# Transposing query and key rows before they are split, two heads at a time

## The chip, the cores and the metric

The kernel runs on one core of a Trainium2 chip. Its engines work side by side: TensorE (PE in the profile; its weight loads are shown apart as PEld), VectorE (DVE), ScalarE (ACT), GpSimd (POOL), and SyncE (SP), whose queue issues the transfers. The metric is the device time of one execution in microseconds (us). Three runs of the kernel before took 1815.14 to 1818.62 us, with a median of 1815.4 us.

## The reference

Two layers of a generator work on 256 latent tokens and 256 context tokens of width 1024, in float32. Each layer is a half-step SwiGLU feed-forward, a token mixing and a second half-step feed-forward, each behind an RMS norm with a shift and a scale that come from a conditioning vector:

```python
x = x + 0.5 * mx[2] * swiglu(modulate(rms_norm(x), mx[0], mx[1]), *ffn1)
h = modulate(rms_norm(x), mx[3], mx[4])
y, y_c = mix_window_diff(...) if l % 2 == 0 else mix_mla_neighbourhood(...)
x = x + mx[5] * y
x = x + 0.5 * mx[8] * swiglu(modulate(rms_norm(x), mx[6], mx[7]), *ffn2)
```

Layer 0 mixes by windowed attention (8 query heads over 2 key heads) and differential attention (4 heads with two queries and keys each); layer 1 by latent attention (8 heads) and neighbourhood attention (8 heads). What matters here is how queries and keys come to the scores, in the windowed, the differential and the neighbourhood attention: each head of 64 columns is normed on its own, and for the latent tokens of layer 0 turned by a rotary embedding, and the score is the dot product of a query row with a key row:

```python
aq = apply_rope2d(rms_norm(aq.reshape(B, S, A_HEADS, HEAD_DIM), a_q_norm), *rope)
s = jnp.einsum('bqhgd,bkhd->bhgqk', qg, k).astype(jnp.float32) * (d ** -0.5)
```

## The kernel before

TensorE multiplies operands of type fp32r, a rounded form of float32. To keep the precision, the kernel splits an operand into a high part (the value rounded to fp32r, a copy on ScalarE) and a low part (value minus high part, on VectorE); `split` (lines 98 to 100) does both, and `mm3` (line 105) multiplies high by high, high by low and low by high. Weights come from memory in blocks `raw` and are split into `hs` by `wcols`; for 21 items named in the table `POOL` the low part is made by GpSimd instead (lines 275 and 276).

Activations stand transposed (features on partitions, tokens along the row) in `xT`. A projection such as `pbk` or `paq` gives two blocks of 128 tokens by four heads in PSUM. `head_norm` squares (ScalarE, line 619), sums (VectorE, line 621), takes the inverse root (line 128 and following, on both engines) and multiplies by it, and with gains and tables makes `tk`, on VectorE. `head_rows` then makes from `tk` the rows that the scores read: head dimension on partitions, tokens along the row. Since a head has only 64 columns, high part and low part of one head stand one above the other on the 128 partitions of one row tile, and one matmul over 128 partitions sums two of the products. A second tile of the keys holds the two halves swapped, for the other two products; queries need none.

Before, `head_rows` splits `tk` while tokens are still on partitions (line 651, two calls), then transposes high and low part of each head together (line 659, one transpose per head and token block, four of them into one PSUM bank of the tag `tr`, of which there are two), copies the bank to the row tile (line 664, or line 662 for the items in `ROWS_DVE`) and makes the swapped tile from the same bank (lines 667 and 669, or 671 for items that are not in `SWAP_ACT`). It runs 18 times with four heads and twice with two (`ak0`, `ak1`): 14 times in the mixing of layer 0, some 405 to 640 us, and 6 times in that of layer 1, some 1386 to 1600 us. The tile names are `bqt`, `bkt`, `aqt`, `akt`, `aktw`, `dqt`, `dkt`.

The items of a mixing stage are recorded in the order of a table written by hand (`MIX0`, `MIX1`). A scheduler then fixes each engine's order for good when the kernel is built, by when it takes the operands to be ready and buffers to be free; on the chip each engine takes its instructions in that order and waits where an operand isn't there.

The last feed-forward (layer 1) reads `hTl`: `raw_chunk` scales the rows of one chunk of `xT` (line 372) and splits them (line 373) as soon as the mixing has finished that chunk. Its first call also writes two columns 256 and 257 that hold the shift (lines 368 and 369), so that the same matmuls give the shift's part.

## Time and profile before

| | |
|---|---|
| median of three runs | 1815.4 us (1815.14 to 1818.62) |
| the profiled execution | 1815.7 us, span 1813.6 us |
| TensorE busy | 1762.3 us, 97% |
| VectorE busy | 1220.6 us, 67% |
| ScalarE busy | 738.8 us, 41% |
| GpSimd busy | 46.0 us, 3% |
| transfers | 256.9 MB, 142 GB/s on the mean |

The span runs from the first to the last instruction that the profiler saw; the execution's own time is 2.1 us longer. A busy time counts each moment once, even where instructions of one engine overlap, so that the mean duration of an instruction times its count can be more than the busy time. "Idle before" is what an engine waited ahead of a group of instructions, with the instruction that ended the wait. Granted clock is the share of TensorE's full 2.4 GHz that it was given in a stretch; its lower level is 1.2 GHz, 0.50.

### The profile page before, as it was taken

What the parts mean: (1) busy time and instruction counts of PE and PEld (TensorE: products, weight loads), DVE (VectorE), ACT (ScalarE), POOL (GpSimd) and SP (SyncE); (2) the same over time, 40 slices, a digit from 0 to 9 for tenths busy, and PEclk for the clock granted to TensorE, in tenths of its full rate; (3) what the DMA queues carried; (4) which work ended last, traced back from release to release, by engine and by line L of the source; (5) the groups of instructions that cost most, each with busy time, mean ns of one, the idle gap of its engine ahead of it and who ended that gap; (6) DMA issues with size and microseconds to landing.
All of it is one profiled execution on the core that took longest, in us unless ns stands there. A gap on an engine that the chain in (4) does not pass through costs nothing.

```text
span 1813.6 us, 26777 instructions
## 1 busy us (share of the span) xinstructions
PE 1762.3 (97%) x10563; PEld 1537.5 (85%) x10563; DVE 1220.6 (67%) x2343; ACT 738.8 (41%) x1322; POOL 46.0 (3%) x25
## 2 busy tenths in 40 slices
PE   7999999999999989999999999999999998999999
PEld 5788888898998888888888988888889986789998
DVE  5999953467688699989854633333346787876664
ACT  4333132345666543222233332222334656664442
POOL 0000000011010000000000000000001011000000
PEclk9999999999999989999999999999999999999999
DMA  9777752322110237778863233233233442155552
GB/s 305 273 245 225 236 190 88 116 73 68 50 60 14 59 121 240 241 229 261 300 199 105 81 94 94 92 105 103 88 111 101 89 102 57 47 178 183 175 186 82
DMA packets 214025, 256.90 MB, mean 142 GB/s; under 512 B 21484, under 2 KB 195724, under 8 KB 213900
## 3 DMA queue, kind: packets, MB, share of 16 engines
q1 hardware_dynamic: 213900, 255.19, 45.6%
q8 instruction: 83, 1.36, 0.3%
q14 instruction: 42, 0.34, 0.1%
HBM read 254.11 MB, written 1.05 MB: 141 GB/s over the span
## 4 chain that ended last, share of the span: by engine, by line
PE 87%; DVE 7%; ACT 3%; DMA 2%; issue 1%; SPq 0%; DVEq 0%; ACTq 0%
PE ups L103 23%; PE gps L103 23%; PE dps L103 23%; PE ops L103 3%; PE po L756 2%; PE sc L103 2%; DVE hs L100 1%; DMA bias<-in_d_rpb_dram 1%; PE trp L659 1%; PE pbk L103 1%; PE pbv L103 1%; PE paq L103 1%; PE pbq L103 1%; PE ptl L724 1%; PE mps L524 1%
## 5 line engine op out<-in xcount | busy, mean ns | idle before, releaser
L100 DVE TENSOR_TENSOR hs<-raw,hs 128x1024 fp32r<-128x1024 f32 (+2 forms) x308 | 367.9, 1200 | 284.1 <-ACT hs L99 283.4
L99 ACT ACTIVATE hs<-raw 128x1024 fp32r<-128x1024 f32 (+2 forms) x308 | 314.9, 1030 | 541.4 <-PE dps L103 177.8
L103 PE MATMUL dps<-ah,hs 128*128 128x512 f32 (+1 forms) x2256 | 401.0, 338 | 0.2 <-DVE hs L100 0.2
L103 PEld LDWEIGHTS dps<-ah,hs 128*128 128x128 f32 x2256 | 350.6, 190 | 46.4 <-DVE hs L100 0.4
L103 PE MATMUL gps<-hT,hs 128*128 128x512 f32 (+1 forms) x1680 | 375.3, 380 | 4.9 <-ACT hT L542 2.7
L103 PE MATMUL ups<-hT,hs 128*128 128x512 f32 (+1 forms) x1680 | 371.6, 377 | 0.0
L103 PEld LDWEIGHTS gps<-hT,hs 128*128 128x128 f32 x1680 | 305.0, 190 | 65.5 <-ACT hT L542 3.5
L103 PEld LDWEIGHTS ups<-hT,hs 128*128 128x128 f32 x1680 | 303.3, 188 | 58.8 <-issue 1.0
L212 DVE CUSTOM_DVE_ANT_0 junk<-mraw,cb,const 128x1024 f32<-128x1024 f32 x224 | 283.6, 1283 | 16.3 <-DMA mraw<-in_k_w_modT_dram 11.1
L99 ACT ACTIVATE ah<-af 128x512 fp32r<-128x512 f32 (+1 forms) x88 | 50.4, 574 | 127.5 <-DVE af L93 93.9
L295 DVE SCALAR_TENSOR_TENSOR xT<-dps,const,xT 128x256 f32<-128x256 f32 x112 | 50.3, 480 | 77.0 <-PE dps L103 76.9
L276 POOL TENSOR_TENSOR hs<-raw,hs 128x1024 fp32r<-128x1024 f32 (+2 forms) x21 | 45.8, 2186 | 1558.2 <-ACT hs L275 1493.8
L93 DVE TENSOR_TENSOR af<-sg,ups 128x512 f32<-128x512 f32 x66 | 45.2, 685 | 41.0 <-PE ups L103 40.9
L103 PE MATMUL gps<-hTl,hs 128*128 128x258 f32 x528 | 66.8, 284 | 1.6 <-DVE hTl L373 1.0
L428 ACT ACTIVATE sg<-gps 128x512 f32<-128x512 f32 x66 | 38.9, 589 | 70.2 <-PE gps L103 70.2
L103 PEld LDWEIGHTS gps<-hTl,hs 128*128 128x128 f32 x528 | 64.7, 190 | 2.5 <-DVE hTl L373 1.2
L103 PE MATMUL ups<-hTl,hs 128*128 128x258 f32 x528 | 65.5, 283 | 0.0
L103 PEld LDWEIGHTS ups<-hTl,hs 128*128 128x128 f32 x528 | 64.4, 190 | 0.0
L100 DVE TENSOR_TENSOR ah<-af,ah 128x512 fp32r<-128x512 f32 (+1 forms) x88 | 54.6, 621 | 13.2 <-ACT ah L99 13.2
L684 DVE TENSOR_REDUCE nm<-sc 128x1 f32<-128x512 f32 (+1 forms) x80 | 53.8, 682 | 5.0 <-PE sc L103 4.6
L690 ACT ACTIVATE pr<-sc,nm 128x512 f32<-128x512 f32 (+1 forms) x64 | 40.3, 634 | 13.7 <-DVE nm L684 13.4
L304 ACT ACTIVATE sq<-xT 128x256 f32<-128x256 f32 (+1 forms) x54 | 23.6, 449 | 50.9 <-DVE xT L295 50.6
(296 smaller groups left out, 1894.3 us busy)
## 6 DMA issues: line engine op xcount, KB each, us to landing
mraw<-in_k_w_modT_dram SPq DMA_DIRECT2D x128, 512.0 KB, 4.6
raw<-in_ffn_w_gate_dram SPq DMA_DIRECT2D x88, 512.0 KB, 4.7
raw<-in_ffn_w_up_dram SPq DMA_DIRECT2D x88, 512.0 KB, 4.5
raw<-in_ffn_w_down_dram SPq DMA_DIRECT2D x80, 512.0 KB, 4.1
raw<-in_cd_w_in_dram SPq DMA_DIRECT2D x18, 512.0 KB, 3.8
wm<-in_w_mod_dram SPq DMA_DIRECT2D x16, 512.0 KB, 8.7
raw<-in_ab_w_in_dram SPq DMA_DIRECT2D x16, 512.0 KB, 3.8
raw<-in_ffn_w_down_dram SPq DMA_DIRECT2D x16, 256.0 KB, 2.7
```

Of the source, the lines that this page charges most:

```text
L93: V.tensor_tensor(out=out_, in0=a, in1=b, op=ALU.mult)
L99: S.activation(h, src, AF.Copy)
L100: V.tensor_tensor(out=l, in0=src, in1=h.bitcast(F32), op=ALU.subtract)
L103: T.matmul(ps, a, b, start=start, stop=stop)
L212: V.tensor_tensor_reduce(out=junk, in0=raw, in1=mod_c[v], scale=0.5 if m in (2, 8) else 1.0, scalar=bT[:, l, m, k:k + 1], op0=ALU.mult, op ...
L276: nc.gpsimd.tensor_tensor(out=hs[:, 1, :n], in0=raw[:, :n], in1=hs[:, 0, :n].bitcast(F32), op=ALU.subtract)
L295: V.scalar_tensor_tensor(out=xT[dc][:, a:e], in0=ps[:, a:e], scalar=modT[:, l, v, m, dc:dc + 1], in1=xT[dc][:, a:e], op0=ALU.mult, op1=ALU ...
L304: S.activation(sq[:, cols], xT[dc][:, cols], AF.Square)
L428: S.activation(sg, g[:, :ntok], AF.Silu)
L684: V.tensor_reduce(out=nm[:, c], in_=view, axis=AX.X, op=ALU.max, negate=True)
L690: S.activation(p[:, cols], sc[:, cols], AF.Exp, bias=nm[:, i + b:i + b + 1], accum_out=den[:, i + b:i + b + 1])
L756: T.matmul(po[64 * x:64 * x + 64, q], val(x, c), pts[x][c], start=c == order[0], stop=c == order[-1], tile_position=(0, 64 * x))
```

## The change

`head_rows` no longer splits `tk`. It transposes `tk` itself, two neighbouring heads (128 columns) at a time, one transpose per pair of heads and token block; all of a call's transposes go into one PSUM bank. After a transpose the first head of a pair stands on partitions 0 to 63, the second on 64 to 127. For each of the two (x), the high part is copied from PSUM to the same partitions of the row tile, and VectorE subtracts it from PSUM into the other half. The second head of a pair so has its high part on the upper 64 partitions, where the first has its low part there, in queries and keys alike. The swapped tile is now copied from the row tile in SBUF, one head and one half at a time, no longer from PSUM.

In `raw_chunk` the first chunk's scaling is issued first, and the shift columns' copies are ordered behind it (`issue_after`).

```diff
         if not hraw:
             hraw.append(hp.tile([P, KC, 2, 264], R32, tag="hTl", name="hTl", bufs=1))
+        h, x, sc = hraw[0][:, k, :, 0:256], xT[k][:, 0:256], modT[:, l, 0, m + 1, k:k + 1]
+        first = S.activation(h[:, 0], x, AF.Copy, scale=sc).ins
+        if len(hraw) == 1:
+            hraw.append(first)
             sh = modT[:, l, 0, m, :].rearrange("p (k o) -> p k o", o=1)
             for c in (256, 257):
-                S.activation(hraw[0][:, :, 0, c:c + 1], sh, AF.Copy)
+                with tc.issue_after(first):
+                    S.activation(hraw[0][:, :, 0, c:c + 1], sh, AF.Copy)
                 V.tensor_tensor(out=hraw[0][:, :, 1, c:c + 1], in0=sh, in1=hraw[0][:, :, 0, c:c + 1].bitcast(F32),
                                 op=ALU.subtract)
-        h, x, sc = hraw[0][:, k, :, 0:256], xT[k][:, 0:256], modT[:, l, 0, m + 1, k:k + 1]
-        S.activation(h[:, 0], x, AF.Copy, scale=sc)
...
-        head_norm(tv, src, gain, rope, sq)
-        spf = []
-        for b in range(2):
-            sp = sq if b == 0 else w2("sp")
-            spv = sp[:, :nh * P].rearrange("p (h s e) -> p h s e", s=2, e=HD)
-            split(spv[:, :, 0, :].bitcast(R32), spv[:, :, 1, :].bitcast(R32), tv[:, b])
-            spf.append(sp)
+        head_norm(tk[:, :2 * nh * HD].rearrange("p (b h e) -> p b h e", b=2, e=HD), src, gain, rope, sq)
+        pt = bank("tr", "trp")
         for i in range(nh // 2):
-            pt = bank("tr", "trp")
+            for b in range(2):
+                T.transpose(pt[:, 256 * i + b * P:256 * i + (b + 1) * P], tk[:, (b * nh + 2 * i) * HD:(b * nh + 2 * i + 2) * HD],
+                            idm)
+        for i in range(nh // 2):
+            d = dst_of(i)
             for x in range(2):
-                for b in range(2):
-                    h = 2 * i + x
-                    T.transpose(pt[:, 256 * x + b * P:256 * x + (b + 1) * P], spf[b][:, P * h:P * h + P], idm)
-            rows = pt.rearrange("p (x n) -> p x n", x=2)
-            if now[0] in ROWS_DVE.split():
-                V.tensor_copy(dst_of(i), rows)
-            else:
-                S.activation(dst_of(i), rows, AF.Copy)
+                own, other = (slice(0, 64), slice(64, 128))[::1 - 2 * x]
+                r = pt[own, 256 * i:256 * i + 256]
+                if now[0] in ROWS_DVE.split():
+                    V.tensor_copy(d[own, x], r)
+                else:
+                    S.activation(d[own, x], r, AF.Copy)
+                V.tensor_tensor(out=d[other, x], in0=r, in1=d[own, x].bitcast(F32), op=ALU.subtract)
             if swap_of is not None:
-                d = swap_of(i)
-                S.activation(d[0:64], rows[64:128], AF.Copy)
-                if now[0] in SWAP_ACT.split():
-                    S.activation(d[64:128], rows[0:64], AF.Copy)
-                else:
-                    V.tensor_copy(d[64:128], rows[0:64])
+                e = swap_of(i)
+                for x in range(2):
+                    own, other = (slice(0, 64), slice(64, 128))[::1 - 2 * x]
+                    S.activation(e[other, x], d[own, x].bitcast(F32), AF.Copy)
+                    if now[0] in SWAP_ACT.split():
+                        S.activation(e[own, x], d[other, x].bitcast(F32), AF.Copy)
+                    else:
+                        V.tensor_copy(e[own, x], d[other, x].bitcast(F32))
```

The scheduler orders the changed program anew. On TensorE, at the start of the first mixing stage, this is the order of before, from the first key projection (`pbk`; `pbv` and `pbq` are other projections, `trp` the transposes; x69 is 69 in a row):

```order
L103 MATMUL pbk<-hs,hT 128x256 x69
L103 MATMUL pbv<-hw,hT 128x256 x15
L103 MATMUL pbk<-hs,hT 128x256 x2
L103 MATMUL pbv<-hw,hT 128x256
L659 MATMUL trp<-const,hsq 128x128 x2
L103 MATMUL pbv<-hw,hT 128x256
L659 MATMUL trp<-const,sp 128x128
L659 MATMUL trp<-const,hsq 128x128
L659 MATMUL trp<-const,sp 128x128 x2
L659 MATMUL trp<-const,hsq 128x128
L659 MATMUL trp<-const,sp 128x128
L103 MATMUL pbv<-hw,hT 128x256 x2
```

Behind these stand 25 of `pbk`, 29 of `pbv` and 6 of `pbq` up to the second group of eight transposes, then 65 of `pbq` up to the third. On TensorE, from the same projection on, the changed kernel has:

```order
L103 MATMUL pbk<-hs,hT 128x256 x68
L103 MATMUL pbv<-hw,hT 128x256 x5
L655 MATMUL trp<-const,tk 128x128 x4
L103 MATMUL pbk<-hs,hT 128x256
L103 MATMUL pbv<-hw,hT 128x256 x7
L103 MATMUL pbk<-hs,hT 128x256 x2
L103 MATMUL pbv<-hw,hT 128x256 x17
L103 MATMUL pbk<-hs,hT 128x256 x25
L103 MATMUL pbv<-hw,hT 128x256 x19
L103 MATMUL pbq<-hs,hT 128x256 x5
L655 MATMUL trp<-const,tk 128x128 x4
L103 MATMUL pbq<-hs,hT 128x256 x28
```

The groups have four transposes in place of eight; the first stands 14 projection matmuls earlier, the second 1, and the third, which follows the last row, 38.

On VectorE, this is what stood before, from the product that begins the norm of the second rows (`ht<-pbk`) to their split (`hsq`, `sp`; `hs<-raw` is a weight block):

```order
L93 TENSOR_TENSOR ht<-pbk,hrs 128x512
L100 TENSOR_TENSOR hs<-raw,hs 128x1024
L93 TENSOR_TENSOR hsq<-ht,const 128x512
L93 TENSOR_TENSOR tk<-ht,const 128x8x16 x4
L96 TENSOR_TENSOR tk<-tk,hsq 128x512
L100 TENSOR_TENSOR hsq<-tk,hsq 128x4x64
L100 TENSOR_TENSOR sp<-tk,sp 128x4x64
```

And this stands on VectorE at the same place now (`bqt` are the rows of the call before, line 666 their low parts):

```order
L666 TENSOR_TENSOR bqt<-trp,bqt 64x256
L663 CAST bqt<-trp 64x256
L93 TENSOR_TENSOR ht<-pbk,hrs 128x512
L666 TENSOR_TENSOR bqt<-trp,bqt 64x256
L93 TENSOR_TENSOR hsq<-ht,const 128x512
L93 TENSOR_TENSOR tk<-ht,const 128x8x16 x4
L100 TENSOR_TENSOR hs<-raw,hs 128x1024
L96 TENSOR_TENSOR tk<-tk,hsq 128x512
```

The split is gone from the end, the weight block has moved to just before the last sum, and low parts of the preceding rows stand between the steps of the norm.

On ScalarE, at the end of the second mixing stage, before (`const<-xT` and `sq` are squares for the next norm):

```order
L275 ACTIVATE hs<-raw 128x1024
L301 ACTIVATE const<-xT 128x256
L372 ACTIVATE hTl<-xT,const 128x256
L304 ACTIVATE sq<-xT 128x256
L372 ACTIVATE hTl<-xT,const 128x256
```

and on ScalarE at this place in the changed kernel:

```order
L275 ACTIVATE hs<-raw 128x1024
L301 ACTIVATE const<-xT 128x256
L367 ACTIVATE hTl<-xT,const 128x256
L373 ACTIVATE hTl<-const 128x8 x2
L304 ACTIVATE sq<-xT 128x256
L367 ACTIVATE hTl<-xT,const 128x256
```

The two shift columns have come here from a place in the first feed-forward stage behind layer 0's mixing; VectorE's two subtractions for them stand around the first chunk's in the same way. On SyncE's queue, in the second mixing stage, one block of `c_w_uq` now stands in front of twelve transfers of `bias` and not behind them.

## Rows read from the trace of the kernel before

**Rows 1.** The page's first part: busy time, share of the span and instructions of each engine.

```profile
PE 1762.3 (97%) x10563; PEld 1537.5 (85%) x10563; DVE 1220.6 (67%) x2343; ACT 738.8 (41%) x1322; POOL 46.0 (3%) x25
```

**Rows 2.** The page's fourth part: the chain of work that ended last, share of the span by engine.

```profile
PE 87%; DVE 7%; ACT 3%; DMA 2%; issue 1%; SPq 0%; DVEq 0%; ACTq 0%
```

**Rows 3.** Busy times in the two mixing stages: start and end, length, then busy time and count of PE, PEld, DVE, ACT and POOL, the granted clock, the share of the transfers, GB/s.

```profile
405.00:640.00 235.00, 226.86 (x1729) 208.17 (x1729) 182.57 (x465) 145.08 (x354) 12.89 (x6) 0.99 0.18 55
1386.00:1600.00 214.00, 199.53 (x1398) 172.00 (x1397) 163.38 (x420) 134.22 (x334) 20.91 (x10) 0.98 0.37 86
```

**Rows 4.** Who TensorE waited for between 385 and 1625 us: us in total, times, longest.

```profile
PE trp L659 <- DVE hsq L100: 9.7, 7, 2.4
PE kvt L1107 <- DVE ckv L1103: 4.8, 1, 4.8
```

**Rows 5.** The transposes of line 659: shortest, median and longest duration in ns, first and last start.

```profile
L659 PE MATMUL trp<-const,hsq x76: 270/273/448, 417.2 to 1472.4; 128*128 128x128 f32 x76
...
L659 PE MATMUL trp<-const,sp x76: 270/273/421, 417.5 to 1472.5; 128*128 128x128 f32 x76
```

**Rows 6.** The chain that ended last in order of time, first mixing stage: start, length in us, what.

```profile
427.91 1.94 PE trp L659 x8
...
447.62 0.87 PE trp L659 x8
...
572.76 0.87 PE trp L659 x8
```

**Rows 7.** Groups of instructions by shape, ScalarE: line, output and input, shapes, count, busy us and mean ns of one, idle time before.

```profile
L99 ACT ACTIVATE ah<-af 128x256 fp32r<-128x256 f32 x22 | 9.1, 412 | 33.4 <-DVE af L437 30.2 <-PE ups L103 3.2
L99 ACT ACTIVATE hsq<-tk 128x256 fp32r<-128x256 f32 x18 | 7.4, 413 | 19.7 <-DVE tk L93 10.2 <-DVE tk L96 9.5
...
L99 ACT ACTIVATE ckt<-cktr 96x256 fp32r<-96x256 f32 x16 | 5.4, 374 | 1.6 <-PE cktr L1213 1.6
L664 ACT ACTIVATE dkt<-trp 128x512 fp32r<-128x512 f32 x8 | 4.8, 598 | 2.6 <-PE trp L659 2.5
...
L667 ACT ACTIVATE dkt<-trp 64x512 fp32r<-64x512 f32 x8 | 4.8, 595 | 0.1
```

**Rows 8.** The same, VectorE.

```profile
L100 DVE TENSOR_TENSOR hsq<-tk,hsq 128x256 fp32r<-128x256 f32 x18 | 9.0, 498 | 1.9 <-ACT hsq L99 1.9
L100 DVE TENSOR_TENSOR sp<-tk,sp 128x256 fp32r<-128x256 f32 x18 | 7.5, 419 | 0.0
...
L100 DVE TENSOR_TENSOR ckt<-cktr,ckt 96x256 fp32r<-96x256 f32 x16 | 6.1, 412 | 0.7 <-ACT ckt L99 0.6
L710 DVE TENSOR_SCALAR pra<-pra,rd 128x256 f32<-128x256 f32 x14 | 4.7, 346 | 0.0
L671 DVE CAST dkt<-trp 64x512 fp32r<-64x512 f32 x6 | 4.1, 684 | 4.1 <-ACT dkt L667 4.1
...
L100 DVE TENSOR_TENSOR sp<-tk,sp 128x128 fp32r<-128x128 f32 x2 | 0.6, 290 | 0.0
L100 DVE TENSOR_TENSOR hsq<-tk,hsq 128x128 fp32r<-128x128 f32 x2 | 0.6, 285 | 0.0
```

**Rows 9.** VectorE's instructions in order of time: start, us, what, and idle time before with its releaser.

```profile
413.15 0.89 DVE L93 TENSOR_TENSOR tk<-ht,const 128x128 f32<-128x128 f32 x4
...
423.02 3.10 DVE L93 TENSOR_TENSOR tk<-ht,const 128x128 f32<-128x128 f32 x4
426.16 0.69 DVE L96 TENSOR_TENSOR tk<-tk,hsq 128x512 f32<-128x512 f32 x1
427.34 0.42 DVE L100 TENSOR_TENSOR hsq<-tk,hsq 128x256 fp32r<-128x256 f32 x1 [0.48 <-ACT hsq L99]
```

**Rows 10.** TensorE's instructions in order of time, at three places.

```profile
427.91 0.66 PE L659 MATMUL trp<-const,hsq 128*128 128x128 f32 x2 [2.12 <-DVE hsq L100]
...
538.91 0.44 PE L659 MATMUL trp<-const,hsq 128*128 128x128 f32 x2 [2.45 <-DVE hsq L100]
...
1614.55 3.51 PE L103 MATMUL gps<-hTl,hs 128*128 128x258 f32 x24 [1.02 <-DVE hTl L373]
```

**Rows 11.** GpSimd's instructions in order of time, at two places.

```profile
422.77 2.60 POOL L276 TENSOR_TENSOR hs<-raw,hs 128x1024 fp32r<-128x1024 f32 x1 [31.86 <-ACT hs L275]
...
1466.39 2.42 POOL L276 TENSOR_TENSOR hs<-raw,hs 128x1024 fp32r<-128x1024 f32 x1 [0.45 <-ACT hs L275]
```

**Rows 12.** Busy times in three short stretches, with the columns of rows 3.

```profile
420.00:430.00 10.00, 7.88 (x59) 7.71 (x58) 8.31 (x15) 4.07 (x7) 2.60 (x1) 0.88 0.37 105
...
540.00:550.00 10.00, 10.00 (x71) 9.63 (x69) 7.61 (x19) 5.83 (x16) 0.00 (x0) 0.83 0.09 27
...
1600.00:1618.00 18.00, 16.58 (x132) 15.81 (x131) 18.00 (x36) 12.56 (x24) 2.40 (x1) 1.00 0.38 123
```

**Rows 13.** VectorE's casts of line 662, one form: durations in ns, first and last start.

```profile
L662 DVE CAST dqt<-trp x2: 679/680/680, 1467.5 to 1468.8; 128x512 fp32r<-128x512 f32 x2
```

**Rows 14.** The shift columns, lines 368 and 369, with the columns of rows 13.

```profile
L368 ACT ACTIVATE hTl<-const x2: 202/210/217, 906.6 to 906.7; 128x8 fp32r<-128x8 f32 x2
...
L369 DVE TENSOR_TENSOR hTl<-const,hTl x2: 169/169/169, 908.8 to 908.9; 128x8 fp32r<-128x8 f32 x2
```

**Rows 15.** The transfers of `bias`: time in SyncE's queue for one in ns, and how long VectorE waited for them (us, times).

```profile
L1053 SPq DMA_DIRECT2D bias<-in_d_rpb_dram x32: 601/615/1879, 1416.6 to 1494.5; - x32
...
  DMA bias<-in_d_rpb_dram: 6.6, 3
```

1 line of the change is left out of this document (removed).

## The prediction

> **What bounds the kernel now.** I read the page's busy times first: TensorE is busy for 1762.3 of 1813.6 us, VectorE for 67% and ScalarE for 41% [rows 1]. Then the chain that ended last: 87% of it is TensorE work, 7% VectorE, 3% ScalarE [rows 2]. So a microsecond of TensorE work is worth nearly a microsecond wherever no other wait stands behind it, and work on the other two engines is worth something only where TensorE waits for it. The change lies in the two mixing stages, so I asked for these two stretches alone. From 405 to 640 us TensorE is busy 226.86 of 235 us and VectorE 182.57; from 1386 to 1600 us TensorE has 199.53 of 214 us, VectorE 163.38 [rows 3]. Both are still TensorE stages, but with VectorE at 78% and 76% close behind. The waits of TensorE say who it waits for there: the longest entry is the very place of the change, the transposes of query and key rows (`trp`) behind the second half of the split on VectorE: 9.7 us, 7 times [rows 4].
>
> **Transposes.** `head_rows` runs 18 times on four heads and twice on two. Each run made two transposes per head, one per token half: 18 x 8 + 2 x 4 = 152, which the trace shows as 76 + 76 [rows 5]. Two heads now go through one transpose, so 76 stay and 76 go, with their weight loads. Eight of them in a row take 0.87 us in the chain at full clock, 0.109 us each; right behind a wait the same eight took 1.94 us, 0.24 each [rows 6]. At 0.109: 52 fewer in the first mixing stage, 5.7 us, and 24 fewer in the second, 2.6 us. I count them by the share of these stages in which TensorE has work (96.5% and 93.2%, [rows 3]): 5.5 + 2.4 = **-7.9 us**. Ends: 0, if the next instruction waits anyway, and -18 (76 x 0.24).
>
> **The split.** What goes on ScalarE: 40 copies of 64 columns by four heads (36 at 0.40 to 0.41, 4 at about 0.3: 15.9 us), 33 row copies of 512 columns at 0.598 (19.7) and 25 swap copies at 0.595 (14.9), in all 50.5 us. What comes: 66 copies of 64x256 out of PSUM, which the trace shows nearly so as `ckt<-cktr` 96x256 at 0.374 (24.7), and 50 swap copies of 64x256 from SBUF, nearest `ah<-af` 128x256 at 0.412 (20.6), in all 45.3 [rows 7]. ScalarE loses 5 us; it is 62% busy in both stages, so this counts as 0.
>
> On VectorE 40 subtractions go (9.0 + 7.5 + 1.2 us, by the busy times) and 16 casts of 512 columns at 0.684 (10.9): 28.6 us. There come 76 subtractions out of PSUM, 6.1 us for 16 in `ckt<-cktr`, 0.38 each (29.0), 10 copies out of PSUM, taken at the same 0.38 (3.8), and 22 swap copies of 64x256 inside SBUF. No row shows those; the nearest is the scaling of 128x256 in place, 4.7 us for 14, 0.336 each (7.4) [rows 8]. That is 40.2 us, so VectorE gains **11.6 us** of work, some 8 of it in the first stage. What hides it is TensorE's own work on projections and outputs; VectorE then stands at about 81% and 78%. Cost on the path: between 0 and +11.6; I take **+1.0**, nearer to 0, because the new work stands behind the transposes, not in front of them, and its readers, the scores, come 9 (last key item of the second stage) to 63 matmuls (first stage) later in TensorE's order.
>
> **The wait before the transposes.** In the trace of before, the sum `tk` ends at 426.85 and the transposes start at 427.91: 1.06 us for copy and subtraction, which no longer stand between [rows 9, 10]. That would be 7 x 1.06 = 7.4 us if every such wait shrank. I take 0, with -7.4 as the other end. The order is why: TensorE's queue is fixed, and the transposes have been moved forward in it. Counted from the first `pbk` matmul, the three first groups stood behind 87, 150 and 215 projection matmuls and now stand behind 73, 149 and 177. Where they arrive earlier, they ask earlier for `tk`. At the second place `tk` itself isn't earlier: the weight split `hs` (1.23 us) that stood in front of the chain now stands inside it, before the last sum, and four subtractions with four copies of the preceding rows (8 x 0.38 = 3.0 us) replace two subtractions and two casts (2.2 us) ahead of it.
>
> What stretched that chain is elsewhere. Four products `tk<-ht` took 3.10 us at 423.02 and 0.89 us at 413.15 [rows 9]; a GpSimd subtraction ran from 422.77 to 425.37 [rows 11], and the 2.12 us wait of TensorE follows; the same stands at 538.91 with 2.45 us [rows 10]. After both, the granted clock is a mixture of its two levels of 2.4 and 1.2 GHz: 0.88 in 420 to 430 and 0.83 in 540 to 550 us [rows 12]. The change doesn't touch the GpSimd instructions, so I leave these two waits and their clock as they are.
>
> A stretched chain can also befall the new instructions. A cast out of PSUM wasn't stretched: two `dqt<-trp` took 0.68 us each at 1467.5 and 1468.8 [rows 13] while GpSimd worked from 1466.39 to 1468.81 [rows 11]. By these rows the 76 new subtractions and 16 lost casts are of the unstretched or half unstretched kind, and the 22 swap copies, now SBUF to SBUF, of the exposed kind. GpSimd works for 33.8 of 449 us in the two stages [rows 3], 7.5%, so one or two of 22 copies would meet it, at most 2.4 us each, and three of the 40 removed subtractions no longer do: taken as 0. The Trainium skill, "SBUF — State Buffer", section "SBUF: two separate sides", says that a VectorE instruction in a two-port mode or with two SBUF inputs and a GpSimd instruction lock each other out of a shared port for a whole instruction; that speaks against the swap copies, and the stretched `tk<-ht` agrees with it. By that rule alone the sum would stay within 2 us of mine, in either direction.
>
> **The shift columns.** Two ScalarE instructions (0.21 each) and two on VectorE (0.169) move from 907 us to 1606 us [rows 14], behind the first chunk. From 1600 to 1618 us VectorE has no idle time at all, 18.00 of 18 us [rows 12], and TensorE waits for its last result, 1.02 us at 1614.55 [rows 10]. Two instructions more in that row of work are 0.34 us on the path; taken with their overlap as **+0.3**, ends 0 and +0.8 (all four). At 907 us their absence is worth nothing, since TensorE is the bound there.
>
> **Transfers.** On SyncE's queue one weight load moves ahead of twelve bias transfers (0.615 us each to issue). VectorE waited 6.6 us in three waits for such a transfer [rows 15] without holding TensorE for it. Cost 0, ends -1 and +2.
>
> **Sum.** The profiled execution took 1815.7 us (1813.6 of span and 2.1 around it). 1815.7 - 7.9 + 1.0 + 0.3 = 1809.1. The median shown is 1815.4, 0.3 lower, so I predict **1808.8 us**.
>
> **Rivals.** B: the waits go too. For it: the seven waits are real and 1.06 us of each was the split. Against it: the moved transposes and GpSimd. With four of seven shortened (4.2 us) and one low-clock stretch gone (0.17 of 10 us, 1.7) and no cost on VectorE: 1815.4 - 7.9 - 5.9 + 0.3 = 1802.
>
> C: given back. TensorE arrives 7.9 us earlier at work that VectorE's unchanged chains finish when they did, as at `kvt`, where it waited 4.8 us for VectorE [rows 4]. Then the time stays: 1815.4 + 0.3, about 1815.7. Against it: TensorE's idle time is only 8.1 and 14.5 us in the two stages, so most of its work has no such wait behind it.
>
> D: slower. VectorE becomes the engine that TensorE waits for: the head norms form one chain on it, and the next norm queues behind the subtractions of the preceding rows. If all of the 11.6 us falls in front of a waited result: 1815.4 + 11.6 - 7.9 + 0.3 = 1819.4. It decides as soon as VectorE adds over 8 us to these chains. For it: stretches such as 1600 to 1618 us, where VectorE has no gap. Against it: on average it keeps a fifth free in the mixing stages.
>
> **How the numbers follow.** I give my forecast 0.55 (1805.5 to 1812.5), B 0.15, C 0.17, D 0.13. What this kernel's measurement can tell from no change is 0.2%, 3.6 us, so faster means below 1811.8. Faster: 0.50 of mine and B, 0.65. Same: 0.05 of mine, 0.15 of C, 0.03 of D, 0.23. Slower: 0.02 of C and 0.10 of D, 0.12. The range of 1800 to 1817 takes in B and C and leaves out D and the best end of B.
>
> **What would show it.** Right: 76 `trp` matmuls; TensorE's idle time in the two mixing stages about as before and the stages together some 7 us shorter; the subtraction near 0.41 us and the swap copy inside SBUF near 0.35; the last stream's first matmuls waiting for VectorE a few tenths longer. Wrong: `trp` waits gone (B), new TensorE waits on the subtraction or behind `kvt` and `cqtr` that make up for the transposes (C), or VectorE above 90% in the mixing stages with longer stages (D).

## The result and the profile after

The changed kernel takes 1842.5 us, median of 4 runs (1840.8 to 1843.1), against 1815.4 for the kernel before: a ratio of 1.0144, 95% interval 1.0126 to 1.0161. It is 27 us slower; 1808.8 had been predicted, in a range to 1817. In its profiled execution the page shows the following.

```profile
PE 1773.3 (96%) x10487; PEld 1533.3 (83%) x10487; DVE 1241.4 (67%) x2395; ACT 739.4 (40%) x1340; POOL 45.7 (2%) x25
...
PE 81%; DVE 12%; ACT 3%; DMA 2%; issue 1%; SPq 1%; POOL 0%; DVEq 0%; ACTq 0%
```

TensorE issues 76 matmuls fewer and is busy 11 us longer than in [rows 1]; in the chain that ended last VectorE's share went from 7% [rows 2] to 12%. To see where the time went, I cut both executions at the same instructions: the first `pbq` matmul, the first `gps` of the feed-forward part behind it, the first `pdq`, the first `gps` of the last stream. Five stretches, lengths in us from the start times in the traces:

| kernel | to pbq | mixing 1 | feed-forward | mixing 2 | last |
|---|---|---|---|---|---|
| before | 399.1 | 255.4 | 731.9 | 225.6 | 201.7 |
| changed | 402.5 | 261.6 | 737.7 | 237.3 | 201.8 |

So 18 us were lost in the mixing stages, where 7.9 were to be gained, and 9 us in feed-forward parts that the change doesn't touch. The busy times of the two mixing stages of the changed kernel, and of 200 us of pure feed-forward work, columns as in [rows 3]:

```profile
402.50:664.10 261.60, 237.11 (x1771) 213.60 (x1769) 216.97 (x547) 155.44 (x390) 12.35 (x6) 0.98 0.20 59
1401.80:1639.10 237.30, 215.47 (x1470) 186.13 (x1469) 180.27 (x464) 143.29 (x356) 23.45 (x11) 0.96 0.35 85
...
1100.00:1300.00 200.00, 200.00 (x874) 163.55 (x873) 67.07 (x78) 51.24 (x61) 0.00 (x0) 1.00 0.31 95
```

The same stretches of the kernel before:

```profile
399.10:654.50 255.40, 239.41 (x1822) 219.83 (x1821) 202.08 (x515) 156.00 (x380) 12.89 (x6) 0.98 0.20 60
1386.40:1611.90 225.50, 211.03 (x1493) 183.50 (x1493) 174.88 (x443) 141.79 (x346) 23.16 (x11) 0.98 0.37 89
...
1100.00:1300.00 200.00, 200.00 (x884) 165.59 (x883) 68.03 (x77) 52.10 (x61) 0.00 (x0) 1.00 0.32 97
```

The last row of each is the one to look at twice: TensorE is busy all the time at full clock in both, yet it gets 874 matmuls done in 200 us and not 884. A busy share of 100% hides that some of the matmuls are a little slower. The groups by shape name them, and show the new instructions (TensorE, ScalarE, VectorE):

```profile
L103 PE MATMUL gps<-hT,hs 128*128 128x512 f32 x1488 | 351.3, 393 | 3.8 <-ACT hT L545 2.7 <-DVE hs L100 1.1
...
L655 PE MATMUL trp<-const,tk 128*128 128x128 f32 x76 | 12.9, 293 | 12.0 <-DVE tk L96 5.7 <-DVE tk L93 4.7 <-DVE nm L690 1.4
...
L665 ACT ACTIVATE aqt<-trp 64x256 fp32r<-64x256 f32 x16 | 6.1, 378 | 9.3 <-PE trp L655 4.8 <-DVE aqt L666 4.5
...
L666 DVE TENSOR_TENSOR aqt<-trp,aqt 64x256 fp32r<-64x256 f32 x16 | 6.8, 422 | 1.8 <-ACT aqt L665 1.4
...
L675 DVE CAST dkt<-dkt 64x256 fp32r<-64x256 f32 x12 | 3.5, 289 | 0.4
```

`gps` was 346.5 us and 390 ns before; with `ups` the 512-column matmuls on `hT` cost 10.4 us of TensorE more. The transposes went from 18.6 + 16.7 [rows 5, by busy time] to 12.9 us. Of the waits of TensorE, those that answer to [rows 4]:

```profile
PE kvt L1111 <- DVE ckv L1107: 5.7, 1, 5.7
PE trp L655 <- DVE tk L96: 5.7, 5, 2.6
PE trp L655 <- DVE tk L93: 4.7, 5, 1.7
...
PE pdq L103 <- DVE hs L100: 3.4, 1, 3.4
```

The wait before the transposes stayed (9.7 before, 11.8 in three entries now, the third 1.4 behind `nm`), and a new one is there, `pdq` (a projection of the second mixing stage) behind a weight split on VectorE. So three things had to be explained: the slower feed-forward matmuls, the `pdq` wait, and the mixing stages.

### The profile page after: what moved, and what is told of

Its sections match the earlier page's. It is cut to its first block, busy times and chain, and to the rows that moved or that the text cites. A ratio compares the mean times of both kernels' runs of the same rounds, so it can differ in the third digit from the quotient of the medians.

```text
span 1841.0 us, 26711 instructions
## 1 busy us (share of the span) xinstructions
PE 1773.3 (96%) x10487; PEld 1533.3 (83%) x10487; DVE 1241.4 (67%) x2395; ACT 739.4 (40%) x1340; POOL 45.7 (2%) x25
## 4 chain that ended last, share of the span: by engine, by line
PE 81%; DVE 12%; ACT 3%; DMA 2%; issue 1%; SPq 1%; POOL 0%; DVEq 0%; ACTq 0%
PE ups L103 23%; PE gps L103 23%; PE dps L103 22%; PE ops L103 2%; PE po L760 2%; DVE hs L100 2%; PE sc L103 1%; DVE nm L688 1%; DMA bias<-in_d_rpb_dram 1%; DVE tk L93 1%; PE pdv L103 1%; PE ptl L728 1%; DVE hT L355 1%; PE mps L527 1%; PE paq L103 1%
## 5 line engine op out<-in xcount | busy, mean ns | idle before, releaser
L103 PE MATMUL gps<-hT,hs 128*128 128x512 f32 (+1 forms) x1680 | 379.7, 382 | 4.9 <-ACT hT L545 2.7
L103 PE MATMUL ups<-hT,hs 128*128 128x512 f32 (+1 forms) x1680 | 377.0, 380 | 0.0
L212 DVE CUSTOM_DVE_ANT_0 junk<-mraw,cb,const 128x1024 f32<-128x1024 f32 x224 | 283.6, 1280 | 16.1 <-DMA mraw<-in_k_w_modT_dram 11.9
L103 PE MATMUL gps<-hTl,hs 128*128 128x258 f32 x528 | 66.7, 284 | 1.8 <-DVE hTl L376 1.0
```

The costliest lines, as they stand in the source:

```text
L103: T.matmul(ps, a, b, start=start, stop=stop)
L212: V.tensor_tensor_reduce(out=junk, in0=raw, in1=mod_c[v], scale=0.5 if m in (2, 8) else 1.0, scalar=bT[:, l, m, k:k + 1], op0=ALU.mult, op ...
```

## Experiments

Ratios are against the kernel before, run on the same chip, with 95% intervals. Stage lengths are those of the one execution that was profiled. It can lie 4 us from its kernel's median (e8: 1825.6 against 1829.6), so a stage difference of 2 or 3 us shows little by itself. Byte addresses are the places that the builds gave the tiles; the traces hold none.

**The shift columns alone, and the place of the streamed tiles.** First the smaller of the two edits, by itself (e1).

```diff
 # before, with raw_chunk of the changed kernel
+        first = S.activation(h[:, 0], x, AF.Copy, scale=sc).ins
...
             for c in (256, 257):
-                S.activation(hraw[0][:, :, 0, c:c + 1], sh, AF.Copy)
+                with tc.issue_after(first):
+                    S.activation(hraw[0][:, :, 0, c:c + 1], sh, AF.Copy)
```

> The kernel before with the edit of the shift columns alone; every engine has the order of before, but for the two copies and two subtractions of those columns. What else differs is where tiles lie in on-chip memory: the eight tiles of normalized stream (hT) lie at 121,696 bytes and above in a partition before, and four of the eight lie at 16,512 to 32,895 bytes here, as they do in the changed kernel. Theory A (a 512-column matmul that streams from that low stretch takes longer: 234 ns from start to start in the changed kernel's trace, 226.7 elsewhere): the four feed-forward halves lose what they lost in the changed kernel, 3.4 + 5.8 us, so 1824.5 us, and the mixing stages stand as before. Rival B (the matmuls were slowed by something else in the changed kernel, such as its transfers or the other engines' order): 1815.4 us. Rival C (my prediction's own term for these columns): 1815.7 us.

Measured: 1829.7 us, ratio 1.0062 (1.0050 to 1.0075); 403.9, 253.0, 737.7, 231.5 and 202.5 us. Theory A in size and place for the feed-forward parts (737.7, as in the changed kernel), but the second mixing stage lost 6 us as well, with TensorE's instructions in the order of before one by one, and those of the other engines but for the four of the columns. Two rows of it, and one wait:

```profile
1100.00:1300.00 200.00, 200.00 (x874) 163.50 (x873) 64.95 (x75) 50.61 (x60) 0.00 (x0) 1.00 0.31 95
...
L103 PE MATMUL gps<-hT,hs 128*128 128x512 f32 x1488 | 351.7, 394 | 3.8 <-ACT hT L545 2.7 <-DVE hs L100 1.1
...
PE pdq L103 <- DVE hs L100: 3.2, 1, 3.2
```

Three kernels with a longer xT asked whether the low place is the reason (e2 the changed kernel, e3 the kernel before, e4 the kernel of e1).

```diff
-    xall = xp.tile([P, KC, NTOK], F32, tag="xT", name="xT")
+    xall = xp.tile([P, KC * NTOK + 160], F32, tag="xT", name="xT")[:, :KC * NTOK].rearrange("p (k n) -> p k n", k=KC)
```

> The changed kernel with the residual tile xT made 640 bytes longer, so that it is placed first and takes 16,512 to 33,535 bytes; the four hT tiles then lie at 33,536 to 49,919. The order of instructions is that of the changed kernel but for a few in the first 30 us. Theory A (the place below 32 KB costs): the 9.2 us come back, 1833.3 us, and 512-column matmuls take 226.7 ns from all eight tiles. Rival A2 (it is not the place but the alignment: the four tiles begin at a multiple of 128 bytes, the weights and the other four do not, and that stays so here): 1842.5 us, 234 ns still. Rival B (something else): 1842.5 us.

> The kernel before with the same longer xT: its hT tiles stay high (122,336 bytes and above), and xT itself, which VectorE and ScalarE read and write all the time, moves from 33,408 to 16,512 bytes. A control. Theory A with the effect in the streamed operand of 512-column matmuls alone: 1815.4 us, less the little that two activation tiles at 24,704 cost the kernel before (some 60 matmuls x 6 ns = 0.4 us). If the low stretch costs VectorE and ScalarE as well: up to 10 us slower, with longer instructions on xT.

> The kernel before with the edit of the shift columns and the longer xT: four hT tiles at 33,536 to 49,919 bytes, the other engines' work as before. Theory A: 1815.4 us, the 9.2 us of the shift columns' edit alone gone. Rival A2 (alignment): 1824.5 us. Rival B: the same as the shift columns' edit alone.

Measured: the changed kernel 1843.7 us, 1.0144 (1.0129 to 1.0159); before 1819.8, 1.0011 (1.0002 to 1.0020); before with late shift columns 1830.8, 1.0071 (1.0058 to 1.0083). Theory A fell: from 33,536 bytes on the four tiles are as slow, 233 to 234 ns from start to start on the mean. What they still had in common was that they begin at a multiple of 128 bytes and the weights 96 past one. The next two kernels change nothing but that, with every engine's order word for word the same (e5 the changed kernel, e6 the kernel before).

```diff
-NCONST = 3636
+NCONST = 3648
```

> The changed kernel with the tile of constants 12 columns longer (48 bytes), so that all that lies above it moves up by 32 bytes; every engine's order is that of the changed kernel, instruction by instruction. In the changed kernel four hT tiles begin at a multiple of 128 bytes (16,512, 20,608, 24,704, 28,800) and the other four, the weights and the activations begin 96 bytes past one (162,656; 64,352; 138,080). Here all begin at a multiple of 128. Theory A3 (what costs is that the streamed tile and the weights stand at different offsets within 128 bytes): all 512-column matmuls at 226.7 ns, 9 to 11 us back, about 1832.5 us. Rival A4 (a streamed tile that begins at a multiple of 128 bytes costs, wherever the weights stand): all of gps, ups and dps with 512 columns at 234 ns or so: 4,200 matmuls x 7 ns less the 9.2 us that are there already, about 20 us slower than the changed kernel, 1862 us. Rival B (neither): 1842.5 us, with the four tiles slow as before.

> The kernel before with the same 48 bytes: same order, streamed tiles and weights all at multiples of 128 bytes but for activation tiles that were at 24,704 already. Theory A3: 1815 us, or up to 0.4 us less (the 60 matmuls of the activation tile at 24,704 are fast now). Rival A4: 1845 us (4,200 matmuls x 7 ns). Rival B: 1815.4 us.

Measured: the changed kernel 1834.4 us, 1.0094 (1.0080 to 1.0107), 8 us less (9 by the ratios); before 1818.7, 1.0004 (0.9995 to 1.0013). The changed kernel's rows are back at those of before:

```profile
1100.00:1300.00 200.00, 200.00 (x884) 165.62 (x883) 66.16 (x76) 51.15 (x61) 0.00 (x0) 1.00 0.30 96
...
L103 PE MATMUL gps<-hT,hs 128*128 128x512 f32 x1488 | 346.5, 390 | 3.8 <-ACT hT L545 2.6 <-DVE hs L100 1.1
```

Theory A3 stands: 731.6 us of feed-forward again, and A4 is out, since all tiles now begin at multiples of 128. By the starts of the 512-column matmuls, what they took beyond 226.7 ns each came to 9.5 us in the changed kernel's feed-forward parts, 1.3 before and 0.3 here. Only one difference of offsets, 96 bytes, was run.

**One mixing stage at a time.** With the offset mended, the new rows in one stage and the old ones in the other (e7, e8).

```diff
...
+    def head_rows(*args):
+        (head_rows_new if now[0][0] in "ab" else head_rows_old)(*args)
```

(`in "d"` for the second kernel.)

> The changed kernel with the 48 bytes, and with the rows of the second mixing stage (d) split and transposed as before; so the new rows are in the first mixing stage alone, and the order of the second stage is that of before. If what the changed kernel lost in the first mixing stage (255.4 us before, 261.6 after, +6.2) comes from the rows and their order there, that stage stays at 261.6 and the second at 225.5 us: by theory A3 1815.4 + 6.2 = 1821.6 us. If the loss is carried from one stage to the next (memory places, transfers, clock), the first stage is short or the second long as well. My prediction's own term for this stage was a gain, 52 transposes x 0.109 = 5.7 us: 1809.7 us.

> The same with the new rows in the second mixing stage alone, the first as before. If the loss there (225.5 us before, 237.3 after, +11.8) comes from the rows and the order in that stage: first stage 255.4, second 237.3 us, by theory A3 1827.2 us. If the larger part of it is the granted clock, which in the changed kernel fell to half after each of five waits of this stage (20.5 us at half clock, 6.8 before), the stage's loss goes with those waits: the wait of pdq for the split weights (3.35 us) and four more. My prediction's own term: a gain of 24 x 0.109 = 2.6 us, 1812.8 us.

Measured: 1830.1 us, 1.0065 (1.0052 to 1.0077), stages 261.2 and 233.3; and 1829.6, 1.0063 (1.0050 to 1.0076), stages 253.4 and 237.4. The loss is made in the stage that has the new rows. But old rows in the second stage don't bring 225.6 back; the late shift columns alone give it 231.5 (e1) and 233.2 (e13, below).

**That second stage: a landing buffer.** What differs there without any change of order is again the layout. By the builds, weights land in four buffers by turns in this stage before (154,464, 158,560, 187,232, 191,328) and in three with the late shift columns. SyncE's queue is in order, so bias transfers stand behind weight transfers that wait for a buffer. SyncE in the second stage (starts at 1386.4 us) before:

```profile
1416.59 6.57 SPq L1053 DMA_DIRECT2D bias<-in_d_rpb_dram  x8
1423.26 7.05 SPq L269 DMA_DIRECT2D raw<-in_cd_w_in_dram  x2
1430.40 6.50 SPq L1053 DMA_DIRECT2D bias<-in_d_rpb_dram  x8
```

and with the shift columns alone (starts at 1394.7):

```profile
1429.00 6.34 SPq L1056 DMA_DIRECT2D bias<-in_d_rpb_dram  x8
1440.21 3.97 SPq L269 DMA_DIRECT2D raw<-in_cd_w_in_dram  x2
1444.27 7.32 SPq L1056 DMA_DIRECT2D bias<-in_d_rpb_dram  x8
```

The second group of bias starts 44.0 us into the stage before and 49.6 now; the first is late by 4.1 already. VectorE adds the bias in order ahead of the weight split that `pdq` needs. Its waits for bias in e1, against 6.6 us in three waits before [rows 15]:

```profile
  DMA bias<-in_d_rpb_dram: 15.1, 4
```

Since TensorE's order is the same in both, its lag can be read matmul by matmul. In e1 half a microsecond is gained up to 50 us; then it loses 2.0 us at a `ptl` (a transpose of softmax weights) behind the first of these waits, 3.4 at `pdq` behind the next two, and 2.8 in the projections behind that, at half clock; 1.5 come back at the next transposes, and nothing is lost later. So the late bias is what this stage lost, whatever made it late. A layout can cost this stage elsewhere too: in e3, with xT moved and early shift columns, the second group of bias is in time (44.1 us), but `kvt` waits 7.0 us, 4.8 before, and the stage takes 229.3. The run that asked for a fourth buffer (e12, on e5):

```diff
-UNITS = {"kq": 15, "ot": 6, "pr": 9, "pt": 10, "w2": 8, "wm": 16, "xn": 4, "hT": 8, "raw": 3, "hs": 5, "mraw": 3}
+UNITS = {"kq": 15, "ot": 6, "pr": 9, "pt": 10, "w2": 8, "wm": 16, "xn": 4, "hT": 8, "raw": 4, "hs": 5, "mraw": 3}
```

> The changed kernel with the 48 bytes and one more landing buffer for weights (four asked for in place of three; in the second mixing stage before had four in rotation, at 154,464, 158,560, 187,232 and 191,328, and the changed kernel three). The engines' order changes at some 50 places, the layout too. Theory W (in the second mixing stage weights and with them the bias transfers behind them in SyncE's queue are late because a landing buffer is missing: the second group of bias transfers begins 49.1 us after the stage's start and 44.0 before, and the split of weights that pdq waits for stands behind the bias on VectorE): pdq's wait of 3.3 us goes and what it costs in granted clock, 4 to 6 us in all: 1828 to 1830 us. Rival: the wait stays and it comes out within 2 us of 1834.4.

Measured: 1841.1 us, 1.0138 (1.0123 to 1.0153), stages 264.0 and 241.2. The `pdq` wait is gone, as expected, but a wait of 6.6 us of `trp` for `tk` stands in its place. The bias did not come earlier: its second group starts 50.9 us into the stage (50.0 in e5), and VectorE waits 16.1 us for bias (16.9 in e5). In this stage TensorE's order differs from e5's at 4 places only. So one buffer more, asked for in this way, didn't help; what an early bias is worth in the changed kernel the run doesn't say.

**VectorE's load.** Three runs on what the new rows put on VectorE.

```diff
 # e9: no subtraction, zeros instead
-                V.tensor_tensor(out=d[other, x], in0=r, in1=d[own, x].bitcast(F32), op=ALU.subtract)
+                S.activation(d[other, x], r, AF.Copy, scale=0.0)
 # e10: no row or swap copy on VectorE
-ROWS_DVE = """bv11 uq0 bq00 dq10 bv01 ak0 uk10 cq00"""
+ROWS_DVE = """"""
-SWAP_ACT = """dk01 bk11 bk00 ak0"""
+SWAP_ACT = """bk00 bk01 bk10 bk11 ak0 ak1 dk00 dk01 dk10 dk11"""
 # e11: before, with idle work
+            V.tensor_tensor(out=tk[0:64, 0:256], in0=tk[0:64, 0:256], in1=tk[0:64, 0:256], op=ALU.subtract)
```

> The changed kernel with the 48 bytes (1834.4 us, stages 260.8 and 238.1), and with its 76 subtractions from PSUM left out: ScalarE writes zeros in their place, so the low parts of the query and key rows are missing from the scores. VectorE has 32 us less to do in the two mixing stages, ScalarE some 29 us more. Theory V (what the new rows cost is VectorE's load: 216.8 of 260.8 us busy against 201.7 of 255.4 before): VectorE is under its load of before (about 194 us in the first stage) and the transposes' 5.1 + 1.8 us come through: first stage about 250, second about 230 us, 1834.4 - 19 = 1815 us or less. Rival O (it is TensorE's order and the length of each chain, whatever engine works on it): the stages stay within 3 us of 260.8 and 238.1, 1831 to 1836 us.

> The changed kernel with the 48 bytes and with all copies of rows and all swap copies on ScalarE, none on VectorE: VectorE 12 us less (4.2 us of row copies, 7.9 us of swap copies), ScalarE some 13 us more, the number and order of steps in a chain unchanged. The tiles are laid out anew, so the first four hT tiles may lie elsewhere; all at multiples of 128 bytes as the weights. Theory V: VectorE's load in the first stage is near that of before, so some 60% of the loss goes, 4 to 8 us of it: 1827 to 1830 us. Rival O: 1832 to 1837 us.

> The kernel before with the 48 bytes (1818.7 us, stages 255.3 and 226.1), and with one idle subtraction of 64x256 on VectorE ahead of each of the 38 groups of transposes, into a part of tk that nobody reads again: some 0.43 us each, 11 us in the first mixing stage and 5 us in the second, with no transfer, no chain and no engine that waits for their result. Theory V: most of it comes through, +6 to +11 us and +3 to +5 us: 1828 to 1834 us. Rival O (VectorE has slack, only chains count): up to 2 us in all, 1819 to 1821 us.

Measured: 1837.3 us, 1.0111 (1.0096 to 1.0126); 1836.8, 1.0114 (1.0099 to 1.0129); and the loaded kernel before 1822.3, 1.0036 (1.0022 to 1.0050). First stages, in the same order:

```profile
397.60:662.70 265.10, 237.66 (x1770) 215.81 (x1768) 191.72 (x495) 174.26 (x442) 12.26 (x6) 0.97 0.19 58
```

```profile
399.10:661.10 262.00, 238.26 (x1770) 214.93 (x1769) 211.19 (x531) 160.71 (x406) 12.64 (x6) 0.97 0.19 59
```

```profile
399.80:660.70 260.90, 240.95 (x1822) 219.95 (x1820) 209.86 (x541) 155.51 (x380) 12.43 (x6) 0.98 0.19 59
```

Theory V fell as a full cause: with 25 us less on VectorE the first stage is 4 us longer, not 10 shorter. Neither e9 nor e10 isolates VectorE, though: ScalarE has 19 and 5 us more there, and TensorE's order came out otherwise at some 100 and 60 places. Idle work on VectorE isn't free: in e11 8 us of it go with 5.6 us in the first stage (its order came out otherwise at some 70 places too), and 4.7 us with nothing in the second.

**TensorE's order or the rows.** The order is the scheduler's, so it can be held: a chain of order-only edges through TensorE's instructions of both mixing stages.

```diff
...
+        for a, b in zip(line, line[1:]):
+            tc.add_manual_dep(b, a.name, mybir.DependencyInfo(mybir.DependencyClass.NoSync, mybir.DependencyReason.DATA),
+                              reason="order")
...
+    T.in_order(tc, ORDER0)
+    T.in_order(tc, ORDER1)
```

> The rows of before (split first, then transposed), the shift columns late, the 48 bytes: the base for the next two. From the runs so far (the shift columns alone 1829.7 us, of which the places of the streamed tiles cost 9): about 1821 us, stages 253 to 255 and 231 to 233 us.

> The changed kernel with the 48 bytes, and with TensorE's instructions in the two mixing stages held in the order of before (a chain of order-only edges), each group of the new transposes at the place of the old group's first. Theory O (what the new rows cost is the order that the scheduler made of them: transposes up to 39 matmuls earlier in TensorE's queue than VectorE can serve, and everything behind them): the first stage is at or below the 254 us of the old rows, the second about 229 to 231: 1815 to 1821 us against 1834.4. Rival N (the rows themselves cost it: the longer chain from transpose to copy to subtraction to swap, and VectorE's 20 us): stages near 260.8 and 238.1 still, 1832 us or more. In between: the first stage keeps what a load on VectorE alone cost the kernel before, +5.6 us in the run with idle subtractions, and loses the rest.

> The other way round: the rows of before with TensorE held in the changed kernel's order in the two mixing stages. Theory O: the loss comes with the order. The old transposes, which need the split first, stand as early as the new ones and wait longer still: first stage 261 us or more, second 237 or more, 1833 to 1840 us. Rival N: near the base, 1821 us, with 2 us more at most for transposes that stand some matmuls earlier.

> The new rows in TensorE's order of before, and all row and swap copies on ScalarE (VectorE 12 us less in the two stages). If TensorE's order is the larger cause and VectorE's load the smaller, this is the fastest with the new rows: some 3 to 5 us under the same order with the copies where the changed kernel has them, in the first stage. If the chain through ScalarE is what scores wait for, it is slower than that.

Measured, with the stages:

| rows | TensorE's order | us | ratio | mixing 1, 2 |
|---|---|---|---|---|
| old (e13) | old | 1823.6 | 1.0043 (1.0028 to 1.0058) | 254.9, 233.2 |
| new (e14) | old | 1838.0 | 1.0122 (1.0104 to 1.0140) | 267.1, 232.5 |
| old (e15) | new | 1850.4 | 1.0189 (1.0170 to 1.0208) | 265.0, 248.0 |
| new, copies on ScalarE (e16) | old | 1838.1 | 1.0125 (1.0109 to 1.0140) | 267.5, 234.8 |

The two stages answer differently. In the second, the run fits theory O: the new rows in the old order take 232.5 us, no more than the old rows (e14's profiled execution is 3 us under its median, so this is no closer than 3 us). In the first it falls: 267.1 against 260.8 in their own order and 254.9 for the old rows. And the new order costs the old rows 10 and 15 us. With the copies on ScalarE e16 was to be 3 to 5 us faster than e14; it isn't, with 13 us less on VectorE in the two stages. In the first stage of e14 TensorE waits for what comes behind the transposes (line 700 is the subtraction there), 6.4 us for finished rows in all:

```profile
PE sc L76 <- DVE bqt L700: 3.1, 1, 3.1
```

**Behind the transposes.** So look at one group, rows of four query heads, at 447.5 us in both traces. ScalarE of the kernel before, from the end of the transposes to the finished rows:

```profile
448.21 1.09 ACT L664 ACTIVATE bqt<-trp 128x512 fp32r<-128x512 f32 x2
```

ScalarE of the changed kernel:

```profile
448.38 0.38 ACT L665 ACTIVATE bqt<-trp 64x256 fp32r<-64x256 f32 x1 [2.48 <-PE trp L655]
448.86 0.69 ACT L694 ACTIVATE pr<-sc,nm 128x512 f32<-128x512 f32 x1
...
449.67 0.38 ACT L665 ACTIVATE bqt<-trp 64x256 fp32r<-64x256 f32 x1
...
450.30 0.69 ACT L694 ACTIVATE pr<-sc,nm 128x512 f32<-128x512 f32 x1
...
450.98 0.36 ACT L665 ACTIVATE bqt<-trp 64x256 fp32r<-64x256 f32 x1
...
451.83 0.38 ACT L665 ACTIVATE bqt<-trp 64x256 fp32r<-64x256 f32 x1 [0.39 <-DVE bqt L666]
```

and its VectorE:

```profile
448.86 0.42 DVE L666 TENSOR_TENSOR bqt<-trp,bqt 64x256 fp32r<-64x256 f32 x1
...
449.39 0.68 DVE L688 TENSOR_REDUCE nm<-sc 128x1 f32<-128x512 f32 x1
450.10 0.43 DVE L666 TENSOR_TENSOR bqt<-trp,bqt 64x256 fp32r<-64x256 f32 x1
451.38 0.42 DVE L666 TENSOR_TENSOR bqt<-trp,bqt 64x256 fp32r<-64x256 f32 x1 [0.85 <-ACT bqt L665]
...
451.91 0.68 DVE L688 TENSOR_REDUCE nm<-sc 128x2 f32<-128x512 f32 x1
452.63 0.43 DVE L666 TENSOR_TENSOR bqt<-trp,bqt 64x256 fp32r<-64x256 f32 x1
```

Before, the rows are whole at 449.30. Now eight pieces alternate between two engines, exponentials (`pr`) and maxima (`nm`) of other heads stand between them in both queues, and the last row is whole at 453.06. Over all groups of four heads the time from the end of the last transpose to the last row is 0.8 to 1.1 us before and 4.1 to 6.4 now for queries, 2.9 to 3.4 and 5.0 to 7.4 for keys with their swap copies. Theory L is that this is what the new rows cost; two runs make the row of pieces shorter in the new rows and longer in the old ones.

```diff
 # e17: both pairs of heads in one tile d, r all columns of pt
-                    S.activation(d[own, x], r, AF.Copy)
+                    S.activation(d[own, :, x], r, AF.Copy)
-                V.tensor_tensor(out=d[other, x], in0=r, in1=d[own, x].bitcast(F32), op=ALU.subtract)
+                V.tensor_tensor(out=d[other, :, x], in0=r, in1=d[own, :, x].bitcast(F32), op=ALU.subtract)
 # e18: old rows, copied in four pieces
-                S.activation(dst_of(i), rows, AF.Copy)
+            for x in range(2):
+                for half in (slice(0, 64), slice(64, 128)):
...
+                        S.activation(dst_of(i)[half, x], rows[half, x], AF.Copy)
```

> The changed kernel with the 48 bytes (1834.4 us, stages 260.8 and 238.1), in which 14 of the 18 calls with four heads hold their two pairs of heads in one tile, so that a copy, a subtraction and a swap copy take both pairs at once: per call two copies and two subtractions of 64x512 in place of four and four of 64x256. The layout comes out with all streamed tiles high and with four landing buffers for weights in the second stage, as before. Theory L (what the rows cost is the length of the chain from the last transpose to the last row: 4.1 to 6.4 us for queries and 5.1 to 7.4 for keys in the changed kernel, 0.8 to 1.1 and 2.9 to 3.4 before): the chains of the 14 calls come down to 3 to 5 us, and 4 to 6 us of the first stage's loss come back beside the 6 us that the landing buffer is worth in the second: 1820 to 1826 us, first stage 255 to 257. Rival (number of pieces and length of the chain don't matter): only the landing buffer shows, 1828 to 1830 us, first stage 260 to 262.

> The rows of before with late shift columns and the 48 bytes (1823.6 us, stages 254.9 and 233.2), with each copy of rows from PSUM (128x512) cut in four of 64x256, as the new rows have them; split, transposes, subtractions and swap copies as before. VectorE has almost nothing more to do (3 of the 20 calls copy there), ScalarE some 30 us more in both stages. Theory L: the chain from transposes to rows grows by 1.5 to 3 us per call and the stages with it: first stage 259 to 263 us, second 234 to 238, 1829 to 1836 us. Rival (the chain has slack; what costs is the subtraction on VectorE behind the transposes): within 3 us of 1823.6.

Measured: 1818.1 us, 1.0005 (0.9997 to 1.0014), and 1862.8, 1.0253 (1.0239 to 1.0266). The stages, first of e17:

```profile
398.60:655.90 257.30, 236.68 (x1770) 214.74 (x1768) 212.97 (x527) 151.69 (x362) 12.22 (x6) 0.97 0.19 60
1387.40:1613.00 225.60, 209.25 (x1471) 182.11 (x1470) 178.83 (x445) 140.06 (x336) 23.32 (x11) 0.98 0.36 89
```

and of e18:

```profile
398.70:680.10 281.40, 247.78 (x1822) 225.51 (x1820) 204.16 (x524) 176.24 (x449) 12.09 (x6) 0.95 0.18 55
1411.50:1658.20 246.70, 218.69 (x1494) 190.91 (x1494) 176.69 (x450) 151.85 (x378) 23.95 (x11) 0.95 0.34 82
```

With both pairs at once the first stage loses 257.3 - 254.9 = 2.4 us and not 5.9; the four groups `aqt` end 2.9 to 3.9 us behind their transposes (4.1 to 5.6 before that), and the four `bqt`, which kept their pieces, 4.8 to 6.6 as ever. The second stage is at 225.6 us, without the `pdq` wait: the second group of bias starts 40.6 us into it, and VectorE waits 2.4 us for bias in all. The cut copies of e18 cost the old rows 26.5 and 13.5 us, with VectorE at its load of e13 (204.2 us, 203.1 there). That is far more than theory L had expected, and not by its mechanism: the rows of e18 end 1.9 to 3.2 us behind their transposes for queries and 4.5 to 5.3 for keys, sooner than in the changed kernel, which lost less. Nor does TensorE wait long for finished rows. This is all of it in the first mixing stage, in the changed kernel:

```profile
PE sc L103 <- ACT bkt L673: 0.3, 1, 0.3
```

and, in e18, the last two of these, below the wait for the split ahead of the transposes:

```profile
PE trp L662 <- DVE hsq L100: 10.9, 7, 4.6
...
PE ptc L737 <- ACT bkt L674: 0.6, 1, 0.6
PE sc L103 <- ACT bqt L669: 0.4, 1, 0.4
```

What grows is the sum of TensorE's waits for everything else on VectorE and ScalarE: in the first stage all its waits are 14.6 us before, 23.0 in the changed kernel and 32.1 in e18. So theory L falls too, but for the held order of e14. And both runs came out in another TensorE order, e17 at some 80 places against e5 and e18 at some 110 against e13; since e15 shows that an order alone can cost 10 to 15 us in a stage, neither shows what the number of pieces costs by itself. No version was faster than the kernel before; e17 equals it.

## Why the prediction was wrong

The 27 us fall into three by the runs: 8.1 that the offset costs (1842.5 against 1834.4, e5), 10.8 for the new rows (1834.4 against 1823.6, e13) and 8.2 that the late shift columns still cost with the offset mended (1823.6 against 1815.4); by the ratios 9, 9 and 8. The sum, by its terms:

- **Transposes, -7.9.** Right. From start to start they take 10.8 and 4.5 us in the two stages before and 5.7 and 2.7 after: -6.9.
- **The shift columns, +0.3.** The step that failed worst. As work it holds (last stretch 201.7 and 201.8 us). But the tile `hTl`, 16.9 KB, is alive from their first write on. Written late, it leaves its place free for the earlier stages, and the whole layout is dealt anew. That edit alone has a ratio of 1.0062, some 11 us. Six between the mixing stages (737.7 us in e1, 731.4 in e13 with the 48 bytes) and two before them are the offset of four `hT` tiles; with that mended 1.0043 is left, some 8 us, and that is the second mixing stage (233.2 against 225.6). The three add up to more than 11 because the mixing stages of e13 came out 1.9 and 1.7 us longer than those of e1, in the same order. I had priced four instructions and not asked what a tile's life holds.
- **VectorE, +1.0 of 11.6.** Wrong in the place rather than the load. The subtraction took 0.42 us, not 0.38, and the two stages gained 20 us of VectorE's busy time (14.9 and 5.4), not 11.6. The step that failed is to ask only for the readers of the new rows. They did come late enough: the rows end 2 to 5 us later behind the transposes, yet TensorE waited 0.3 us for them in both stages together. But the new pieces are in-order work ahead of other heads' maxima and norms, and it is for such results that TensorE waits longer: 23.0 us of waits in all in the first stage, 14.6 before. (In the second they are 21.4 and 14.0, the late bias among them.)
- **ScalarE, 0.** The same error: 45 us in place of 50, but 116 short pieces in place of 98, each waiting for its turn. Runs e9 and e18, with 19 and 20 us more of short ScalarE work in a stage where it is busy 60%, lost 4 and 26 us, in other TensorE orders.
- **The wait before the transposes, 0.** Right within 2 us, by its own reason: they ask earlier and `tk` isn't earlier.
- **GpSimd, 0.** Right. One of 22 swap copies met a GpSimd subtraction (1.74 us at 440.52, GpSimd busy from 439.70 to 442.12); the others took 0.29.
- **Transfers, 0.** Wrong in the wait. VectorE waits 14.6 us in six waits for bias in the changed kernel, 6.6 in three before, and `pdq` stands behind two of them, 3.4 us; that such a wait does not hold TensorE is no longer so. It isn't the weight load that moved ahead, since in e1, which has SyncE's order of before, the bias is as late.

Rival D had the sign and named VectorE; it asked for 8 us of it on the chains and gave 1819. Its mark, VectorE above 90% in the mixing stages, is not there: 83% and 76%. The new rows alone, with the offset mended, cost 5.9 us in the first stage and 4.9 in the second (260.8 against 254.9, 238.1 against 233.2), net of the transposes' 6.9. Runs e9 and e10 speak against VectorE's load by itself; e14 speaks for the order that the scheduler made around the new rows, in the second stage.

The clock is part of the second stage's loss. In the changed kernel the trace's record has 20.5 us at 1.2 GHz there in five stretches, each at or right after a wait of TensorE of 0.9 to 5.7 us, against 6.8 us in one before: by those numbers at most 7 us of the 11.8 (half of 13.7), on top of the waits themselves. In the first stage the two are alike, 12.6 and 11.8 us.

Shown by runs: the offset (e1, e2, e4, e5); that the layout alone costs the second stage, through late bias (e1, e13); that the new rows cost their own stage (e7, e8). Only argued: that the missing landing buffer is what made the bias late, since e12 did not bring it forward and e17 changed the rows as well; and that the new rows cost what they put back in the queues of ScalarE and VectorE, since TensorE's waits say so but no run holds TensorE's order and changes the pieces alone. Open: how much of that is the number of pieces and how much the order that came with them; and what the offset meets in the memory.

## What to carry to other kernels

Price an edit of a few small instructions by what it does to the lives of tiles too: compare the layout of both builds, the offset of streamed tiles against weights, and how many buffers each rotation has. Where a large instruction is replaced by short ones that alternate between two engines, ask not only when their own result is read, but which other results come later because both queues are in order: here TensorE waited 0.3 us for the new rows and some 8 us more than before, in the first stage, for the rest. Busy shares of 60 to 80% don't say that there is room. And an edit hands the scheduler a new problem: the order that it found for the new rows cost the old ones 27 us.
